# Left operands of the way down summed on VectorE, late differences moved, and attention's convolution and norm in wider instructions

## The chip, the core and the metric

The kernel runs on one core of one Trainium2 chip. The time is that of one execution on the device, in microseconds (us). Before the change the median of three runs was 2420.58 us (2420.09 to 2423.67).

## The reference

One step of a one-layer encoder on two streams: 1024 rows of a new stream, and 64 further rows of a running one that brings 512 cached keys and values, the state of its recurrence, and the last rows ahead of two convolutions. The kernel takes both as T = 1088 columns.

```python
xn = rmsnorm(x)
z, xbc, dt, q, k, v, gate_ssm, gate_att = split(xn @ w_in)
xbc = silu(causal_conv(xbc, 4 taps))                 # 3072 channels
y = ssd_scan(xs, dt, a_neg, bm, cm, state)           # 32 heads, chunks of 64
y = rmsnorm((y + d * xs) * silu(z))
a = softmax(q1 @ k1.T) - lam * softmax(q2 @ k2.T)    # 8 heads, causal by chunks of 64
o = rmsnorm(a @ v, subln_w) * (1 - lambda_init)
x += (sig(gate_ssm) * (y @ w_branch_ssm) + sig(gate_att) * (o @ w_branch_attn)) @ w_out
ha, hb = split(rmsnorm(x) @ w_up)                    # 2 x 2816 channels
x += (silu(causal_conv(ha, 3 taps)) * hb) @ w_down
```

The outputs are x of both streams, the new keys and values, the states, and the last rows ahead of the convolutions, all in float32.

## The kernel before

**How products are made.** Every float32 operand is split into a rounded part hi and a rest lo. A product is then three passes of TensorE: hi by hi, hi by lo, lo by hi, each over a quarter of the columns (QW = 272; HT = 544 is a half). The hi part is a copy on ScalarE (L419), the lo part a subtraction on VectorE (L420); together they are a "split". The large products (input, way up, way down) take two blocks of rows and two halves of the inner dimension at a time and make seven products of them instead of eight. A pair of blocks has 14 steps: product p = 0 to 6, column half s = 0 and 1. For these products both operands need sums and differences of their quadrants:

- The left operands are weights. `make_left` (L551) loads the quadrants of a pair of weight blocks into two buffers (w_f), makes s1 = q21 + q22 (L563), s2 = s1 - q11 (L567), s3 = q11 - q21 (L569) and s4 = q12 - s2 (L565) on GpSimd, and splits what a product needs: wh is a split of products 0 to 3, w_hi and w_lo that of 4 to 6. The rows that s1 and s2 are kept in are named ws1 and ws2. Splits are pinned behind the last evacuation of TensorE's results ("copy" on ScalarE, "read" on VectorE). `lefts_at` says at which of a pair's 14 steps each piece for the next pair is made.
- The right operands are activations of 128 x 1088 elements (a unit of four blocks of 272 columns). In the way down `right_part` loads one of them, and `landed` splits it some steps later, where there are n, m or ph in the rows of the trace. A group of products starts with new right operands.

**The stages.** Input projection with its norm (to about 560 us), attention (560 to 1100), the scan with the products of the branches (1100 to 1560), the output product (to 1730), the way up (1730 to 2160, 22 pairs), and the way down (to 2424, 12 pairs). The way down has three groups of inner blocks, DOWN = (8, 8, 6), with four pairs each; groups are summed up in memory.

**Attention and its filler.** For each of 8 heads there are 9 blocks of 128 query rows (the ninth is the running stream with 64). A block takes: scores on TensorE (sc), a mask and a maximum on VectorE (L1115 or L1116 among them), exponentials on ScalarE (p_t, L1125), the combination of the two softmaxes on VectorE, transpositions on TensorE, copies of them on ScalarE and VectorE (a_t, L1145 and L1147), the product with the values (po, L1160). One block is in flight beside the next one's scores. Between them `fill` puts steps of other products into TensorE's order: the 24 tiles of the scan's input projection with their convolution of four taps (`conv_tiles`, L977), and gates. A tile has four blocks of 272 columns. For each one ScalarE copies the product into pre, makes the first tap (L999), VectorE adds three taps (L1001), then comes silu (L1003) and a store to x_sc in memory. The first three columns of pre come from the block before, by GpSimd (L989). At the end of a head `head_out` scales each of the nine blocks by its norm and by the weight wsub (L1178), transposes them and splits the result (L1189, L1190) into memory. The cached values of the running stream (cv_t) are loaded ahead of a head.

**The way up and down.** In the way up each pair makes a row of h, with a convolution of three taps (L1626 on ScalarE, L1628 on VectorE), and stores it in h_sc. For the way down pairs of rows ("couples") are read back, four differences are made (`differences_of`, L1690: loads at L1694, subtractions at L1698, L1699, L1702 and L1703, stores to t_sc at L1705). Most couples have theirs made in the way up; the last three, whose rows come last, at steps 1, 8 and 10 of the first three pairs of the way down: loads, first two subtractions, other two with the stores. These three are the rows that the third group takes.

`down_pair` (L1720) makes a pair: its passes are L1791, its results are evacuated by ScalarE (products 0 and 2) and VectorE (u at L1796, L1801 and L1805, yq at L1803, L1810 and L1813) and added to the output in memory by GpSimd's DMA queue.

The code gives the order in which work is written. A scheduler then orders it on each engine, with its own estimate of durations and those pins, so a change in one place can move instructions elsewhere.

## Time and profile before

| | |
|---|---|
| runs, median | 2420.58 us (2420.09 to 2423.67) |
| profiled execution, its own time | 2425.83 us |
| its span in the trace | 2424.0 us |
| mean granted clock of TensorE | 0.997 |
| busy: TensorE, VectorE, ScalarE, GpSimd | 98%, 72%, 50%, 30% |
| instructions of the span | 49267 |

A row of a group in the profile reads: line, engine, operation, written tile <- read tiles, size, count; behind the bar the busy time and the mean duration of one in ns; behind the second bar the engine's idle time just before such instructions and what ended most of it. A row of the timeline has the start, the duration and the instruction; in brackets stands the idle time before it and what ended it. A row of waits reads: engine, what waited <- what it waited for, then the sum of us, the count and the longest. Engines are PE (TensorE), PEld (its weight loads), DVE (VectorE), ACT (ScalarE), POOL (GpSimd) and SP (SyncE, which issues most DMAs). The granted clock is a share of full speed.

### The profile page before, as it was taken

The numbers are of one execution on the slowest core, as the hardware profiler recorded it, in microseconds if no ns is written. First come the engines' busy times: TensorE is split into PE (matmuls) and PEld (weight loads), VectorE is DVE, ScalarE is ACT, GpSimd is POOL, SyncE is SP. The second block draws the span as 40 slices with busy tenths as digits, with TensorE's granted clock in tenths as the row PEclk, the third lists the DMA queues.
The fourth block names the chain that finished last, engine by engine and source line by source line (L and its number), as shares of the span: only waits on it lengthen the run. The fifth ranks groups of instructions, "written<-read, shape, count | busy, mean of one in ns | idle before, by whom it ended". The sixth has DMA issues, their size and how long they took to land.

```text
span 2424.0 us, 49267 instructions
## 1 busy us (share of the span) xinstructions
PE 2379.3 (98%) x18648; PEld 2306.1 (95%) x18648; DVE 1750.6 (72%) x3150; ACT 1217.8 (50%) x2695; POOL 731.4 (30%) x773
## 2 busy tenths in 40 slices
PE   8999999999999999999999999999999999999998
PEld 8999999999999999999888899999999999999998
DVE  4678987646868778884789776656866767677765
ACT  6454454325656666665666564334543334352442
POOL 0032433321101101111444442012254455444444
PEclk9999999999999999999999999999999999999999
DMA  7773868536555544435978955764124424367976
GB/s 240 274 245 129 265 218 303 168 104 205 163 157 153 164 143 135 143 104 180 352 264 267 344 190 186 210 208 142 66 82 157 143 98 160 127 199 200 245 182 105
DMA packets 295087, 449.78 MB, mean 186 GB/s; under 512 B 36601, under 2 KB 188290, under 8 KB 294850
## 3 DMA queue, kind: packets, MB, share of 16 engines
q1 hardware_dynamic: 265506, 387.00, 49.5%
q0 software_dynamic: 11040, 26.34, 5.5%
q10 hardware_dynamic: 18304, 33.30, 3.7%
q8 instruction: 146, 2.39, 0.4%
q14 instruction: 91, 0.75, 0.1%
HBM read 294.03 MB, written 152.50 MB: 184 GB/s over the span
## 4 chain that ended last, share of the span: by engine, by line
PE 44%; DVE 6%; DMA 3%; issue 2%; ACT 1%; POOL 1%; SPq 0%; POOLq 0%; DVEq 0%; ACTq 0%
PE mx L1617 13%; PE mx L1791 6%; PE mm L1617 5%; PE mm L170 2%; PE mm L172 2%; PE mm L171 2%; PE mx L170 2%; PE mm L1791 2%; PE mx L172 2%; PE mx L171 2%; PE yi L1306 1%; PE stp L1318 1%; PE ye L1312 1%; DMA b<-y_sc 1%; DMA m_sc<-b_g 1%
## 5 line engine op out<-in xcount | busy, mean ns | idle before, releaser
L170 PE MATMUL mm<-b,w_hi 128*128 128x272 f32 x1376 | 408.7, 297 | 0.0
L172 PE MATMUL mm<-b,w_lo 128*128 128x272 f32 x1376 | 404.2, 294 | 0.0
L171 PE MATMUL mm<-b,w_hi 128*128 128x272 f32 x1376 | 403.0, 293 | 0.0
L170 PEld LDWEIGHTS mm<-b,w_hi 128*128 128x128 f32 x1376 | 259.5, 189 | 5.7 <-issue 3.4
L171 PEld LDWEIGHTS mm<-b,w_hi 128*128 128x128 f32 x1376 | 259.6, 189 | 4.5 <-issue 3.1
L172 PEld LDWEIGHTS mm<-b,w_lo 128*128 128x128 f32 x1376 | 259.1, 188 | 3.6 <-issue 2.5
L1617 PE MATMUL mx<-m,w_hi 128*128 128x272 f32 x792 | 152.3, 290 | 1.2 <-ACT m L419 1.2
L420 DVE TENSOR_TENSOR wh<-w_f,wh 128x512 fp32r<-128x512 f32 (+1 forms) x156 | 151.6, 973 | 0.7 <-ACT wh L419 0.7
L1001 DVE SCALAR_TENSOR_TENSOR cc<-pre,par,cc 128x272 f32<-128x272 f32 (+1 forms) x288 | 139.6, 488 | 9.8 <-ACT cc L999 7.5
L1617 PE MATMUL mx<-n,wh 128*128 128x272 f32 x1056 | 141.6, 288 | 1.1 <-DVE u L1644 1.1
L1125 ACT ACTIVATE p_t<-sc,mx 128x512 f32<-128x512 f32 (+6 forms) x144 | 106.2, 740 | 67.5 <-DVE mx L1116 37.4
L1617 PEld LDWEIGHTS mx<-n,wh 128*128 128x128 f32 x1056 | 135.7, 188 | 1.3 <-DVE u L1644 1.3
L989 POOL COPY pre<-pre 128x3 f32<-128x3 f32 x72 | 27.7, 385 | 346.3 <-DVE cc L1003 182.1
L563 POOL TENSOR_TENSOR ws<-w_f 128x512 f32<-128x512 f32 (+1 forms) x51 | 69.3, 1360 | 198.2 <-DMA w_f<-in_win_dram 82.0
L1617 PEld LDWEIGHTS mx<-m,w_hi 128*128 128x128 f32 x792 | 124.4, 188 | 1.4 <-ACT m L419 1.4
L170 PE MATMUL mx<-b,w_hi 128*128 128x272 f32 x416 | 122.9, 296 | 2.0 <-ACT w_hi L155 1.5
L172 PE MATMUL mx<-b,w_lo 128*128 128x272 f32 x416 | 121.5, 294 | 0.0
L171 PE MATMUL mx<-b,w_hi 128*128 128x272 f32 x416 | 121.4, 292 | 0.0
L1617 PE MATMUL mx<-m,w_lo 128*128 128x272 f32 x396 | 114.2, 289 | 0.0
L1626 ACT ACTIVATE cc<-pre,par 128x544 f32<-128x544 f32 (+1 forms) x44 | 37.2, 846 | 146.2 <-DVE pre L1661 145.3
L156 DVE TENSOR_TENSOR w_lo<-w_f,w_hi 128x1024 fp32r<-128x1024 f32 (+1 forms) x74 | 92.8, 1256 | 22.5 <-ACT w_hi L155 22.1
L419 ACT CAST wh<-w_f 128x512 fp32r<-128x512 f32 (+1 forms) x156 | 95.2, 613 | 27.0 <-POOL w_f L569 8.3
(463 smaller groups left out, 7311.7 us busy)
## 6 DMA issues: line engine op xcount, KB each, us to landing
w_f<-in_win_dram SPq DMA_DIRECT2D x40, 512.0 KB, 4.3
w_f<-in_wup_dram SPq DMA_DIRECT2D x80, 256.0 KB, 2.9
w_f<-in_win_dram SPq DMA_DIRECT2D x76, 256.0 KB, 3.3
bc<-a_sc SPq DMA_DIRECT2D x32, 512.0 KB, 7.1
b<-y_sc SPq DMA_DIRECT2D x24, 544.0 KB, 8.1
h_sc<-hb SPq DMA_DIRECT2D x44, 272.0 KB, 2.1
ht<-h_sc SPq DMA_DIRECT2D x22, 544.0 KB, 4.7
t_sc<-ht SPq DMA_DIRECT2D x22, 544.0 KB, 2.9
```

The costliest lines, as they stand in the source:

```text
L156: V.tensor_tensor(out=lo, in0=w, in1=hi, op=ALU.subtract)
L170: PE.matmul(ps, a_hi, b_hi, start=i == 0, stop=False)
L171: PE.matmul(ps, a_hi, b_lo, start=False, stop=False)
L172: PE.matmul(ps, a_lo, b_hi, start=False, stop=i == n - 1)
L419: S.copy(hi, src)
L420: V.tensor_tensor(out=lo, in0=src, in1=hi, op=ALU.subtract)
L563: G.tensor_tensor(out=s1, in0=q21, in1=q22, op=ALU.add)
L1001: V.scalar_tensor_tensor(cc[:, :m], pre[:, i : i + m], cw(i), cc[:, :m], ALU.mult, ALU.add)
L1125: act(p_t[:n, :nk], sc[c][:n, :nk], AF.Exp, bias=mx[:n, c : c + 1], accum_out=dst)
L1617: PE.matmul(ps, w[x][:, c], b[y][:, k], start=start and k == i == 0, stop=k == 3 and i == 2, skip_group_check=not start)
L1626: act(cc[:, :n], pre[h][:, :n], AF.Identity, bias=col(O_FB + f), scale=cw(0))
L1791: PE.matmul(ps, w[y][:, c], b[z][:, k], start=start and k == j == 0, stop=k == n - 1 and j == 2, skip_group_check=not start)
```

## The change

Five edits, the first two in the way down and the others in attention:

1. For the first pair of each group of the way down (`by_vector`: left operands 22, 26 and 30) the four sums and differences s1 to s4 are made on VectorE, pinned behind the last "copy" and "read", instead of on GpSimd without a pin.
2. The late couples' steps are no longer 1, 8 and 10 in each of the first three pairs, but 5, 11, 13 in the first, 4, 10, 12 in the second and 2, 8, 10 in the third (`LATE`).
3. The convolution of the scan's input works on halves of 544 columns: two blocks of the product are copied into one pre, and then come one first tap, three taps, one silu and one store. pre has two buffers as before, cc two instead of three, each of about twice the size.
4. cv_t has one buffer instead of two, and the cached values of the heads after the first are loaded when the fourth block of the head begins, not before its first.
5. In `head_out` the norm of eight blocks is one multiplication of 128 x 1024 with a broadcast, and a small one for the ninth block. The weight is transposed into a column once (one transposition on TensorE, one copy of a column on ScalarE), and is applied when the transposed rows are split: as the scale of the hi copy on ScalarE and as a factor in the lo subtraction on VectorE.

```diff
+LATE = ((5, 11, 13), (4, 10, 12), (2, 8, 10))
...
-            if what == "s1":
-                G.tensor_tensor(out=s1, in0=q21, in1=q22, op=ALU.add)
...
+            if x in by_vector:
+                with after("copy", "read"):
+                    V.tensor_tensor(out=to, in0=a, in1=b, op=op)
             else:
-                G.tensor_tensor(out=q21, in0=q11, in1=q21, op=ALU.subtract)
+                G.tensor_tensor(out=to, in0=a, in1=b, op=op)
...
+                first = c % HT == 0
+                if first:
+                    pre = cv_pool.tile([P, HT + 6], F32, name="pre", tag="pre", bufs=2)
...
-                cc = cv_pool.tile([P, QW + 3], F32, name="cc", tag="cc", bufs=3)
...
+                if first:
+                    return
...
+                cc = cv_pool.tile([P, HT + 3], F32, name="cc", tag="cc", bufs=2)
...
-            cv_t = ak.tile([P, 4, P], F32, name="cv_t", tag="cv_t", bufs=2)
+            cv_t = ak.tile([P, 4, P], F32, name="cv_t", tag="cv_t")
...
-                cached()
+            later.append(cached)
...
-            for i in range(9):
-                n = min(P, T - i * P)
-                V.scalar_tensor_tensor(o_t[:n, i], o_t[:n, i], rs[:n, i : i + 1], wsub[:n], ALU.mult, ALU.mult)
+            V.tensor_tensor(out=o_t[:, :8], in0=o_t[:, :8], in1=rs[:, :8].unsqueeze(2).to_broadcast([P, 8, P]), op=ALU.mult)
+            V.tensor_scalar(o_t[:TS, 8], o_t[:TS, 8], rs[:TS, 8:9], None, ALU.mult)
...
-                S.copy(hi, pt[:, :w])
-                V.tensor_tensor(out=lo, in0=pt[:, :w], in1=hi, op=ALU.subtract)
+                act(hi, pt[:, :w], AF.Copy, scale=wcol)
+                V.scalar_tensor_tensor(lo, pt[:, :w], wcol, hi, ALU.mult, ALU.subtract)
...
+        pw = pa.tile([P, 512], F32, name="pw", tag="pt", bufs=2)
+        PE.transpose(pw[:, :P], wsub, ident)
+        S.copy(wcol, pw[:, 0:1])
...
+                if x == 3 and later:
+                    later.pop()()
...
+    by_vector = [FT + 4 * g for g in range(len(DOWN))]
...
-            if i in (0, 1, 2) and at in (1, 8, 10):
-                if at == 1:
+            if i in (0, 1, 2) and at in LATE[i]:
+                if at == LATE[i][0]:
```

The lines of the changed kernel are shifted: the sums on VectorE are L567, L420 is L421, the way down's L1791 to L1813 are L1803 to L1825, L1628 is L1640, L1651 to L1661 are L1663 to L1673, and L1698 is L1710.

In VectorE's order at the entry to the way down, before, there stand the splits of the first right operands (n9, n5, n11, m001, m011), the reads of the way up's last pairs (hb, u1 and pre), and two splits of left operands, the one from ws2 (the second product's) and the one from w_f:

```order
L1661 TENSOR_TENSOR pre_27144<-mx_27232,u2_27148 128x272
L420 TENSOR_TENSOR n9_27190<-n9_27190,n8_27189 128x1088
L420 TENSOR_TENSOR n5_27211<-n5_27211,n4_27210 128x1088
L1651 TENSOR_TENSOR u1_27147<-mm_27309,u1_27147 128x272
L420 TENSOR_TENSOR n11_27228<-n11_27228,n10_27227 128x1088
L420 TENSOR_TENSOR wh_27366<-ws2_27282,wh_27366 128x512
L1653 TENSOR_TENSOR hb_27146<-mx_27374,u1_27147 128x272
L420 TENSOR_TENSOR m001_27247<-m001_27247,m000_27246 128x1088
L1655 TENSOR_TENSOR hb_27145<-mx_27394,u1_27147 128x272
L420 TENSOR_TENSOR wh_27388<-w_f_22175,wh_27388 128x512
L420 TENSOR_TENSOR m011_27266<-m011_27266,m010_27265 128x1088
```

At the same place of VectorE's order in the changed kernel:

```order
L1673 TENSOR_TENSOR pre_26612<-mx_26700,u2_26616 128x272
L567 TENSOR_TENSOR ws1_26749<-w_f_21642,w_f_21643 128x512
L421 TENSOR_TENSOR n9_26658<-n9_26658,n8_26657 128x1088
L421 TENSOR_TENSOR n5_26679<-n5_26679,n4_26678 128x1088
L567 TENSOR_TENSOR ws2_26750<-ws1_26749,w_f_21642 128x512
L567 TENSOR_TENSOR w_f_21642<-w_f_21642 128x512
L1663 TENSOR_TENSOR u1_26615<-mm_26777,u1_26615 128x272
L421 TENSOR_TENSOR n11_26696<-n11_26696,n10_26695 128x1088
L421 TENSOR_TENSOR m001_26715<-m001_26715,m000_26714 128x1088
L1665 TENSOR_TENSOR hb_26614<-mx_26842,u1_26615 128x272
L1667 TENSOR_TENSOR hb_26613<-mx_26862,u1_26615 128x272
L421 TENSOR_TENSOR m011_26734<-m011_26734,m010_26733 128x1088
```

Three sums (s1 into ws1, s2 into ws2, s3 into w_f) have come between the splits of right operands, and the split from ws2 has moved from behind n11 to behind m011 and a tap of the last convolution.

On TensorE, where the way down begins in the changed kernel (L1803; L1629 is the way up's last pair), the first product's twelve passes come first, six passes that take the other right operands' tiles for the first time, and the last twelve passes of the way up's last pair:

```order
L1803 MATMUL mx<-ph,wh 128x272 x12
L1803 MATMUL mx<-n_26639,wh 128x272
L1803 MATMUL mx<-n_26640,wh 128x272
L1803 MATMUL mx<-n_26657,w_hi 128x272
L1803 MATMUL mx<-n_26658,w_hi 128x272
L1803 MATMUL mm<-m_26714,w_hi 128x272
L1803 MATMUL mm<-m_26715,w_hi 128x272
L1629 MATMUL mx<-m_21322,w_hi 128x272
L1629 MATMUL mx<-m_21323,w_hi 128x272
```

Before, the twelve passes were followed at once by the rest of the product with n. Six passes and the end of the way up have moved ahead of it.

VectorE's order around the first late couple (ht), before:

```order
L1810 TENSOR_TENSOR yq_27537<-mx_27489,u_27450 128x272
L420 TENSOR_TENSOR n7_27349<-n7_27349,n6_27348 128x1088
L1628 SCALAR_TENSOR_TENSOR cc_27149<-pre_27144,par_81,cc_27149 128x546
L1796 TENSOR_TENSOR u_27451<-mx_27594,u_27450 128x272
L1698 TENSOR_TENSOR ht_27485<-ht_27485 128x544
L1803 TENSOR_TENSOR yq_27554<-mm_27541,u_27450 128x272
L1805 TENSOR_TENSOR u_27451<-mm_27541,u_27451 128x272
```

The same place of VectorE's order in the changed kernel:

```order
L1822 TENSOR_TENSOR yq_27001<-mx_26953,u_26918 128x272
L421 TENSOR_TENSOR n7_26817<-n7_26817,n6_26816 128x1088
L1815 TENSOR_TENSOR yq_27018<-mm_27005,u_26918 128x272
L1817 TENSOR_TENSOR u_26919<-mm_27005,u_26919 128x272
L421 TENSOR_TENSOR m201_26838<-m201_26838,m200_26837 128x1088
L1646 TENSOR_TENSOR hb_26614<-hb_26614,cc_26617 128x480
L1646 TENSOR_TENSOR hb_26614<-hb_26614,cc_26617 128x64
```

The difference (L1698, now L1710) no longer stands ahead of the reads yq and u; it comes nine instructions further on.

VectorE's order at the entry to the second group in the changed kernel, from the last reads of the first group (yq and u) to the second product's split (wh from ws2):

```order
L1825 TENSOR_TENSOR yq_27798<-mx_27785,u_27661 128x272
L567 TENSOR_TENSOR ws1_27800<-w_f_21642,w_f_21643 128x512
L567 TENSOR_TENSOR ws2_27801<-ws1_27800,w_f_21642 128x512
L1808 TENSOR_TENSOR u_27661<-mm_27826,u_27660 128x272
L421 TENSOR_TENSOR ph_27685<-ph_27685,ph_27684 128x1088
L567 TENSOR_TENSOR w_f_21642<-w_f_21642 128x512
L421 TENSOR_TENSOR wh_27840<-w_f_21642,wh_27840 128x512
L421 TENSOR_TENSOR n1_27703<-n1_27703,n0_27702 128x1088
L421 TENSOR_TENSOR wh_27879<-ws2_27801,wh_27879 128x512
```

The other rows stand as before; the three sums have come into them. The fourth (s4) comes eleven rows on, behind the splits of n5 and n11; before, GpSimd made it beside the split of n5.

43 lines of the change are left out of this document (22 added, 21 removed).

## The prediction

> **What bounds the kernel now.** I read the profile from the whole to the single wait: busy times, stages, what TensorE waits for in each stage, and the instructions behind those waits.
>
> ```profile
> PE 2379.3 (98%) x18648; PEld 2306.1 (95%) x18648; DVE 1750.6 (72%) x3150; ACT 1217.8 (50%) x2695; POOL 731.4 (30%) x773
> ```
>
> TensorE is busy for 98% of the span, 2424.0 - 2379.3 = 44.7 us are left. VectorE and ScalarE are not the bound, so what the change takes from them counts only where TensorE stands still for them. The busy time by stage (window, its length, busy us and count of PE, PEld, DVE, ACT, POOL, then the granted clock) shows where that is.
>
> ```profile
> 560.00:1100.00 540.00, 537.24 (x4116) 515.05 (x4115) 432.38 (x1046) 347.00 (x941) 67.39 (x164) 1.00 0.49 150
> 1100.00:1560.00 460.00, 449.60 (x3606) 410.09 (x3606) 337.35 (x464) 263.82 (x619) 163.56 (x108) 1.00 0.78 255
> 1730.00:2160.00 430.00, 430.00 (x3423) 429.97 (x3422) 292.82 (x492) 167.38 (x307) 217.70 (x247) 1.00 0.37 124
> 2160.00:2424.00 264.00, 250.08 (x1952) 248.04 (x1950) 188.27 (x291) 102.92 (x179) 110.85 (x99) 0.98 0.79 197
> ```
>
> Attention (560 to 1100) leaves TensorE 2.8 us idle, the scan 10.4, the way up 0.0, the way down with the drain of the last stores 13.9. The change touches attention and the way down, and through the scheduler the scan's order. The waits of TensorE, in the same order of stages:
>
> ```profile
> PE sc L1111 <- ACT p_t L1125: 1.1, 1, 1.1
> PE po L1160 <- ACT a_t L1145: 0.9, 2, 0.6
> PE po L1160 <- DVE a_t L1147: 0.5, 1, 0.5
> ...
> PE yi L1306 <- DVE y L1314: 3.1, 2, 1.6
> PE tr L1285 <- DVE xx L1294: 2.3, 3, 1.4
> ...
> PE mm L1791 <- DVE n L420: 1.9, 1, 1.9
> PE mm L1791 <- DVE u L1805: 1.5, 1, 1.5
> PE mx L1791 <- DVE u L1796: 0.4, 1, 0.4
> ```
>
> In the way down all waits are for VectorE, and they cost more than they last. Two stretches around them, and one of the way up for comparison (window, length, busy and count of PE, granted clock):
>
> ```profile
> 2171.30:2197.30 26.00, 23.84 (x168) 0.93 0.74 223
> 2264.00:2274.00 10.00, 8.14 (x53) 0.83 1.11 287
> 1740.00:1766.00 26.00, 26.00 (x208) 1.00 0.29 95
> ```
>
> Undisturbed, 208 passes take 26.0 us, 0.125 us each. At the entry to the way down (2171 to 2197) only 168 ran, 40 x 0.125 = 5.0 us late; at the entry to its second group 53 instead of 80, 3.4 us late. Of this the lower clock took 26 x 0.07 = 1.8 us and 10 x 0.17 = 1.7 us. So a wait of 1.5 or 1.9 us brought a second loss of about its own size. [...] In the scan, waits of up to 1.6 us left it at 1.00, so it doesn't always fall.
>
> **Second group: the sums on VectorE.** VectorE, then GpSimd, then TensorE around 2260 us:
>
> ```profile
> 2255.65 2.15 DVE L420 TENSOR_TENSOR ph<-ph 128x1088 fp32r<-128x1088 f32 x1
> ...
> 2262.69 1.27 DVE L420 TENSOR_TENSOR n<-n,n 128x1088 fp32r<-128x1088 f32 x1
> ...
> 2265.53 2.40 DVE L420 TENSOR_TENSOR n<-n,n 128x1088 fp32r<-128x1088 f32 x1
> ...
> 2268.21 0.68 DVE L420 TENSOR_TENSOR wh<-w_f,wh 128x512 fp32r<-128x512 f32 x1
> ```
>
> ```profile
> 2256.73 2.23 POOL L567 TENSOR_TENSOR ws<-ws,w_f 128x512 f32<-128x512 f32 x1
> ...
> 2265.18 1.60 POOL L565 TENSOR_TENSOR w_f<-w_f,ws 128x512 f32<-128x512 f32 x1
> ```
>
> ```profile
> 2267.99 0.39 PE L1791 MATMUL mm<-n,w_hi 128*128 128x272 f32 x1 [1.86 <-DVE n L420]
> ```
>
> A split of 128x1088 takes 1.27 us alone and 2.40 beside a GpSimd sum: VectorE loses 1.1 us for each sum that it meets. The split that TensorE waits for is the one that met the fourth sum (L565). In the change that sum is behind it on VectorE, so the split ends 1.1 us earlier. The other three sums come before; each costs VectorE about 0.6 us (0.68 for a split of the same 512 columns, some 0.08 of it overlapped with the next) instead of 0.9 to 1.1 us of standstill, and VectorE had idle time ahead of the product's read at 2262.34, so their sign hardly counts. The wait falls from 1.86 to about 0.7 us, and I take it that the clock then holds: 1.2 + 1.7 = **2.9 us** gained (bounds: 1.2 if the clock falls all the same, 3.4 if all goes). [...]
>
> **First group: gain and loss.** The rows of VectorE and TensorE at the entry:
>
> ```profile
> 2166.75 2.48 DVE L420 TENSOR_TENSOR n<-n,n 128x1088 fp32r<-128x1088 f32 x2
> ...
> 2170.95 0.69 DVE L420 TENSOR_TENSOR wh<-ws,wh 128x512 fp32r<-128x512 f32 x1
> ...
> 2175.25 1.83 DVE L1628 SCALAR_TENSOR_TENSOR cc<-pre,par,cc 128x544 f32<-128x544 f32 x1
> ...
> 2180.77 0.78 DVE L1628 SCALAR_TENSOR_TENSOR cc<-pre,par,cc 128x544 f32<-128x544 f32 x1
> ...
> 2190.95 1.44 DVE L1698 TENSOR_TENSOR ht<-ht 128x544 f32<-128x544 f32 x1
> 2192.31 0.43 DVE L1803 TENSOR_TENSOR yq<-mm,u 128x272 f32<-128x272 f32 x1
> 2192.66 0.42 DVE L1805 TENSOR_TENSOR u<-mm,u 128x272 f32<-128x272 f32 x1
> ```
>
> ```profile
> 2172.83 1.66 PE L1791 MATMUL mx<-n,wh 128*128 128x272 f32 x12
> ...
> 2193.14 0.73 PE L1791 MATMUL mm<-ph,wh 128*128 128x272 f32 x2 [1.54 <-DVE u L1805]
> ```
>
> The gain: the wait of 1.54 us ends with u (L1805), and the first difference of a late couple (L1698, 1.44 us) stands two instructions ahead of it. In the change it has moved behind the pair yq, u: 1.4 us. The cc of 2175.25 no longer meets a sum, 1.0 us (1.83 against 0.78).
>
> The loss: the split of the second operand (wh from ws), which the second product needs from its third pass on, ends at 2171.64 now. In the change's order, from the end of the read at 2166.75, VectorE has four sums and splits of 512 columns up to and with it (4 x 0.6), five of 1088 (5 x 1.2), three reads (3 x 0.36) and one cc (0.7): 2.4 + 6.0 + 1.1 + 0.7 = 10.2 us, so it ends at about 2176.9. TensorE has 12 passes, then 6, then 12 of the last up pair before it must have it, 30 x 0.125 after 2171.3, so at about 2175.1 (2175.5 with the three passes that also stand ahead): a new wait of **1.4 us**. Adding up the rest of VectorE's list in the same way, TensorE meets two more waits of 0.5 to 0.8 us before it starts the next pair, and is 2.4 to 2.9 us late there instead of 5.0, with the clock held. I take **2.3 us** gained; the bounds are 4.0 (everything but 1 us) and a loss of 1.4 (the new wait in full, nothing given back).
>
> Third group: its only wait is the 0.4 us above. Nothing is counted, within 0.4 us either way. Of the couples' moved steps also the loads (SP's queue) go later; what they write is read again two pairs on, from 2243 us, more than 30 us behind the last step of the first couple, so this is hidden.
>
> **Attention.** VectorE's and ScalarE's groups, with the mean ns of one behind the comma, those of the way up with the doubled width, and a 128x1024 of VectorE:
>
> ```profile
> L1001 DVE SCALAR_TENSOR_TENSOR cc<-pre,par,cc 128x272 f32<-128x272 f32 x213 | 103.4, 487 | 8.9 <-ACT cc L999 7.2
> ...
> L999 ACT ACTIVATE cc<-pre,par 128x272 f32<-128x272 f32 x71 | 43.5, 613 | 8.1 <-DMA x_sc<-cc 3.3 <-POOL pre L989 1.2 <-ACT pre L990 0.4
> ...
> L1178 DVE SCALAR_TENSOR_TENSOR o_t<-o_t,ors,wsub 128x128 f32<-128x128 f32 x56 | 15.4, 342 | 0.1
> ```
>
> ```profile
> L156 DVE TENSOR_TENSOR w_lo<-w_f,w_hi 128x1024 fp32r<-128x1024 f32 x72 | 90.3, 1255 | 22.0 <-ACT w_hi L155 21.6
> ...
> L1628 DVE SCALAR_TENSOR_TENSOR cc<-pre,par,cc 128x546 f32<-128x546 f32 x44 | 37.5, 852 | 1.1 <-ACT cc L1626 0.4
> ...
> L1626 ACT ACTIVATE cc<-pre,par 128x546 f32<-128x546 f32 x22 | 18.6, 846 | 145.3 <-DVE pre L1661 145.3
> ```
>
> The convolution's 96 blocks become 48. Three taps save 3 x 48 x (2 x 0.487 - 0.852) = 17.6 us of VectorE, the first factor 48 x (2 x 0.613 - 0.846) = 18.2 us of ScalarE. The norm's nine products per head (9 x 0.342 = 3.1 us) become one of 128x1024 (1.26 us) and a small one: 8 x 1.6 = 13 us less. The weight rides on the two instructions that split the transposed rows anyway, at no cost that these rows show. But that is some 30 of 432 us on an engine that TensorE waited for 0.5 us here. Only the idle 2.8 us can be won. The longest wait (1.1 us, sc behind p_t, at 1066 us) stands right behind nine norm products; I count that and a part of the rest, **1.5 us** (bounds: 0 and 2.8). Taking cached values at the fourth block into a single buffer costs nothing as long as they land within the five blocks (5 x 540 / 72 = 37 us) that follow. One transposition more at the start is one pass, 0.3 us at most.
>
> **Scan.** No instruction of it changes, but its order on all engines does, since the scheduler starts it from another state. I count 0, with 4 us either way out of its 10.4 us of idle time.
>
> **The sum**: 2.9 + 2.3 + 1.5 = 6.7 us less. The profiled execution took 2425.83 us (span 2424.0), so 2419.1 of such an execution. The median of the runs is 5.25 us below it at 2420.58; carried over, **2413.9 us**. About 0.2% (4.8 us) is what a measurement of this kernel can tell from no change: the marks are 2415.7 and 2425.4.
>
> **The rivals.**
> - *The scan falls better as well* (two of its VectorE waits, 3.1 and 2.3 us, go, or the entry's new wait doesn't arise): 4 us more, 2410. For it: those waits are bare in the trace; against: nothing in the change aims there. 0.2.
> - *VectorE is the bound at both entries and takes the sums' time back*, or the clock falls at the new waits too (2 x 1.7 us): the change does what it says, as the order shows, and gives 2 to 3 us: 2418. For it: between 2166 and 2193 VectorE hardly stands idle. 0.25.
> - *Slower: the wide taps hold softmax back.* A tap lasts 0.36 us longer; an attention block has four VectorE steps in a chain (mask and maximum, reciprocal, combination, copy), each of which finds a tap in front of it about every other time: 4 x 0.5 x 0.36 = 0.7 us later per block. One unit in flight hides it now; if it no longer does in 15 of the 72 blocks, that costs 10 us, and with the gains above, 2424 to 2428, say 2427. It decides from about 15 blocks on. Against it: there are half as many taps, and only five waits now. 0.1.
> - *The forecast*: 0.45, its own range 2411 to 2417.
>
> **Chances.** Faster by over 0.2%: 0.33 of the forecast's 0.45 (the part of its own range below 2415.7), the scan's 0.2 and 0.05 of the second rival's 0.25, together 0.58; within 0.2%: the forecast's other 0.12 and 0.20 of the second rival, 0.32; slower: 0.10. The range leaves out the slowest of the slower case, half of it, and about as much beyond the scan's 2410 - 4: 2406 to 2425.
>
> **What would show it.** Right: no wait for n (L420) above 1 us and a granted clock near 1.00 around the second group's start; a wait for wh (from ws) at the first product pair of about 1.4 us; no wait behind a late couple's difference; idle TensorE time in attention below 2 us. Wrong: a clock still at 0.83 to 0.93 at the entries, more waits for maxima or p_t in attention, or a scan whose idle time differs from 10.4 by more than 4 us.

## The result, and the profile after

The changed kernel takes 2437.90 us (median of six runs, 2434.35 to 2439.68), before takes 2421.47 (six runs, 2420.09 to 2424.81): 1.0064 of before, interval 1.0051 to 1.0077. The medians are 16.4 us apart; by the ratio the change is 0.64% slower, where 6.7 us less was forecast.

The profiled execution has a span of 2436.7 us against 2424.0. Its page, engine by engine (busy us, share, instructions):

```profile
PE 2380.8 (98%) x18649; PEld 2308.3 (95%) x18649; DVE 1729.7 (71%) x2914; ACT 1202.4 (49%) x2600; POOL 682.1 (28%) x713
```

TensorE does the same work, VectorE, ScalarE and GpSimd do less, and the span is 12.7 us longer. (Before's profiled execution, 2425.83 us, was slower than its six runs above, the changed kernel's, 2438.51, was near its median; so the stages add up to 12.7 us and not to 16.4.) To see where, take the first and last instruction of a kind as the ends of a stage: scores (sc) for attention, transpositions of the scan (tr), the way down's first and last passes. Each row gives the count, shortest, median and longest ns, and the first and last start. Before:

```profile
L1111 PE MATMUL sc<-kh,q x208: 191/341/500, 566.0 to 1095.7; 128*128 128x512 f32 x73, 128*128 128x384 f32 x8, 128*128 128x256 f32 x8, 128*64 128x64 f32 x8
...
L1285 PE MATMUL tr<-con,in x144: 270/273/331, 1127.8 to 1464.8; 128*128 128x128 f32 x128, 128*64 128x128 f32 x16
...
L1791 PE MATMUL mx<-ph,wh x135: 282/287/293, 2171.3 to 2404.5; 128*128 128x272 f32 x135
...
L1791 PE MATMUL mx<-m,w_lo x105: 285/290/296, 2184.3 to 2413.9; 128*128 128x272 f32 x105
```

The same rows of the changed kernel:

```profile
L1118 PE MATMUL sc<-kh,q x208: 191/341/501, 564.7 to 1091.2; 128*128 128x512 f32 x73, 128*128 128x384 f32 x8, 128*128 128x256 f32 x8, 128*64 128x64 f32 x8
...
L1297 PE MATMUL tr<-con,in x144: 270/272/476, 1122.4 to 1474.2; 128*128 128x128 f32 x128, 128*64 128x128 f32 x16
...
L1803 PE MATMUL mx<-ph,wh x135: 283/287/293, 2179.3 to 2417.6; 128*128 128x272 f32 x135
...
L1803 PE MATMUL mx<-m,w_lo x105: 284/289/296, 2195.2 to 2427.0; 128*128 128x272 f32 x105
```

Attention went from 529.7 to 526.5 us, 3.2 less. From its last scores to the scan's last transposition it was 369.1 and is 383.0: **13.9 more**. The way down was 242.6 and is 247.7: **5.1 more**. (1.3 less came ahead of attention and 1.4 less between the scan's last transposition and the way down. In seven profiles with the same order of work there, before and e2, e5, e6, e9, e10 and e18 below, these two stretches differ by 4.6 and 2.2 us.) TensorE's longest waits in the changed kernel, from attention on:

```profile
PE tr L1297 <- DVE xx L1306: 4.7, 1, 4.7
PE mx L1803 <- ACT w_hi L420: 4.0, 2, 3.5
PE tr L1297 <- DMA in<-x_sc: 3.9, 1, 3.9
...
PE mx L1803 <- DVE yq L1822: 3.2, 1, 3.2
...
PE mm L1803 <- DVE w_lo L421: 2.0, 1, 2.0
...
PE mx L1803 <- DVE wh L421: 1.2, 1, 1.2
```

The waits that the change was aimed at (n at L420, u behind the late couple) are gone. Others have come, two of them in the scan, of which no instruction was edited.

**The way down.** VectorE, then ScalarE, in the first pair of the second group:

```profile
2277.91 0.68 DVE L567 TENSOR_TENSOR w_f<-w_f,ws 128x512 f32<-128x512 f32 x1
2278.51 0.68 DVE L421 TENSOR_TENSOR w_lo<-w_f,w_hi 128x512 fp32r<-128x512 f32 x1
2279.11 0.68 DVE L421 TENSOR_TENSOR w_lo<-ws,w_hi 128x512 fp32r<-128x512 f32 x1
```

```profile
2283.97 1.10 ACT L420 CAST n<-n 128x1088 fp32r<-128x1088 f32 x1 [4.65 <-DMA n<-h_sc]
...
2286.38 0.61 ACT L420 CAST w_hi<-w_f 128x512 fp32r<-128x512 f32 x1
```

TensorE in the way down:

```profile
2201.36 0.49 PE L1803 MATMUL mx<-m,w_hi 128*128 128x272 f32 x2 [3.23 <-DVE yq L1822]
...
2252.46 0.39 PE L1803 MATMUL mx<-n,wh 128*128 128x272 f32 x1 [1.15 <-DVE wh L421]
...
2279.25 0.40 PE L1803 MATMUL mm<-ph,w_lo 128*128 128x272 f32 x1 [2.00 <-DVE w_lo L421]
...
2287.05 0.52 PE L1803 MATMUL mx<-n,w_hi 128*128 128x272 f32 x2 [3.51 <-ACT w_hi L420]
```

The fourth sum (L567 at 2277.91) no longer stands beside a split that TensorE waits for. But it is late itself, and two operands are made behind it: w_lo, 2.00 us late, and the split of s4. Its hi copy (w_hi from w_f) now stands behind copies of right operands on ScalarE, and ScalarE waited 4.65 us for the DMA of one of them: 3.51 us late, although s4 had been ready for 7.8 us.

VectorE at two other places of the way down, and GpSimd at the same times:

```profile
2195.43 1.46 DVE L1640 SCALAR_TENSOR_TENSOR cc<-pre,par,cc 128x546 f32<-128x546 f32 x1
...
2197.16 1.43 DVE L421 TENSOR_TENSOR wh<-w_f,wh 128x512 fp32r<-128x512 f32 x1
2198.52 2.35 DVE L421 TENSOR_TENSOR m<-m,m 128x1088 fp32r<-128x1088 f32 x1
...
2245.93 3.78 DVE L1711 TENSOR_TENSOR ht<-ht 128x544 f32<-128x544 f32 x1 [1.18 <-DMA ht<-h_sc]
```

```profile
2194.71 1.59 POOL L569 TENSOR_TENSOR ws<-w_f 128x512 f32<-128x512 f32 x1 [18.01 <-DVE hb L1646]
2196.38 1.67 POOL L569 TENSOR_TENSOR ws<-ws,w_f 128x512 f32<-128x512 f32 x1
2198.00 1.71 POOL L569 TENSOR_TENSOR w_f<-w_f 128x512 f32<-128x512 f32 x1
...
2246.28 1.57 POOL L569 TENSOR_TENSOR ws<-ws,w_f 128x512 f32<-128x512 f32 x1
2247.53 1.58 POOL L569 TENSOR_TENSOR w_f<-w_f 128x512 f32<-128x512 f32 x1
```

VectorE comes to the read (yq) that TensorE waits for at 2201 only 21.4 us after the way down's first pass; before it was 15.0 (2186.30 against 2171.3). Ahead of it there are now the four sums of the first pair, and in the new order also the two splits shown, which met the second pair's sums on GpSimd and took 1.43 and 2.35 us where they take 0.68 and 1.28 alone. And a step of the third couple (ht, 0.72 us alone) ran into two sums in a row and took 3.78 us; the 1.15 us at 2252 stand behind it.

**The scan.** From attention's last scores to the last transposition TensorE runs the same 2914 passes, but stands idle for 18.2 us instead of 8.3. The other 4 us are longer busy time, at a granted clock of 0.98 instead of 1.00. Two of VectorE's three longest products of decay and scores, and GpSimd beside them:

```profile
1179.66 4.49 DVE L1310 TENSOR_TENSOR bc<-bc,b_cb 128x1024 f32<-128x1024 f32 x1
...
1289.02 7.62 DVE L1310 TENSOR_TENSOR bc<-bc,b_cb 64x512 f32<-64x512 f32 x1 [0.66 <-issue]
```

```profile
1179.30 3.76 POOL L1345 TENSOR_TENSOR y<-y,zin 128x1536 f32<-128x1536 f32 x1
...
1286.85 3.47 POOL L1345 TENSOR_TENSOR y<-y,zin 128x1536 f32<-128x1536 f32 x1
1290.28 1.04 POOL L1335 TENSOR_TENSOR state<-state,decs 128x512 f32<-128x512 f32 x1
1291.27 1.09 POOL L1307 TENSOR_SCALAR_AFFINE_SELECT bc<-bc 128x1024 f32<-128x1024 f32 x1
1292.33 1.81 POOL L1347 TENSOR_TENSOR zin<-zin 128x768 f32<-128x768 f32 x1
1294.09 1.04 POOL L1335 TENSOR_TENSOR state<-start,decs 128x512 f32<-128x512 f32 x1
1295.09 1.00 POOL L1348 TENSOR_TENSOR zin<-zin 128x384 f32<-128x384 f32 x1
```

VectorE's instruction at 1289.02 lasts 7.62 us, through the six of GpSimd's from 1286.85 on, which run without a gap, and ends 0.5 us after the sixth.

### The profile page after: what moved, and what is told of

Read it like the earlier page. It is cut to its first block, busy times and chain, and to the rows that moved or that the text cites. A ratio compares the mean times of both kernels' runs of the same rounds, so it can differ in the third digit from the quotient of the medians.

```text
span 2436.7 us, 48641 instructions
## 1 busy us (share of the span) xinstructions
PE 2380.8 (98%) x18649; PEld 2308.3 (95%) x18649; DVE 1729.7 (71%) x2914; ACT 1202.4 (49%) x2600; POOL 682.1 (28%) x713
## 4 chain that ended last, share of the span: by engine, by line
PE 50%; DMA 4%; DVE 4%; issue 2%; ACT 1%; POOL 1%; POOLq 0%; SPq 0%; DVEq 0%; ACTq 0%
PE mx L1629 13%; PE mx L1803 5%; PE mm L1629 5%; PE mm L171 4%; PE mm L172 4%; PE mm L173 4%; PE mx L171 3%; PE mx L173 3%; PE mx L172 2%; PE mm L1803 2%; PE yi L1318 1%; PE stp L1330 1%; PE po L1167 1%; PE ye L1324 1%; DMA t_sc<-ht 1%
## 5 line engine op out<-in xcount | busy, mean ns | idle before, releaser
L1629 PE MATMUL mx<-m,w_hi 128*128 128x272 f32 x792 | 152.3, 289 | 1.2 <-ACT m L420 1.2
L421 DVE TENSOR_TENSOR wh<-w_f,wh 128x512 fp32r<-128x512 f32 (+1 forms) x156 | 144.7, 928 | 0.8 <-ACT wh L420 0.7
L1629 PE MATMUL mx<-n,wh 128*128 128x272 f32 x1056 | 141.6, 288 | 1.1 <-DVE u L1656 1.1
L1629 PEld LDWEIGHTS mx<-n,wh 128*128 128x128 f32 x1056 | 135.7, 188 | 1.3 <-DVE u L1656 1.3
L1629 PEld LDWEIGHTS mx<-m,w_hi 128*128 128x128 f32 x792 | 124.4, 188 | 1.4 <-ACT m L420 1.4
L1009 DVE SCALAR_TENSOR_TENSOR cc<-pre,par,cc 128x544 f32<-128x544 f32 (+1 forms) x144 | 111.2, 772 | 8.2 <-ACT cc L1007 6.9
L1629 PE MATMUL mx<-m,w_lo 128*128 128x272 f32 x396 | 114.1, 289 | 0.0
L420 ACT CAST wh<-w_f 128x512 fp32r<-128x512 f32 (+1 forms) x156 | 95.3, 613 | 26.8 <-POOL w_f L569 8.2
L1646 POOL TENSOR_TENSOR hb<-hb,cc 128x544 f32<-128x544 f32 (+2 forms) x63 | 67.1, 1078 | 135.5 <-DVE hb L1667 101.2
```

The source lines that it names most:

```text
L420: S.copy(hi, src)
L421: V.tensor_tensor(out=lo, in0=src, in1=hi, op=ALU.subtract)
L1009: V.scalar_tensor_tensor(cc[:, :m], pre[:, i : i + m], cw(i), cc[:, :m], ALU.mult, ALU.add)
L1629: PE.matmul(ps, w[x][:, c], b[y][:, k], start=start and k == i == 0, stop=k == 3 and i == 2, skip_group_check=not start)
L1646: (V if f + 1 == FT else G).tensor_tensor(out=hb[h][:, o : o + n], in0=hb[h][:, o : o + n], in1=cc[:, d : d + n], op=ALU.mult)
```

## The experiments

All ratios are to the kernel before on the same chip, with their 95% intervals. "Attention", "scan" and "way down" are the three stretches defined above, in us, from one profiled execution each. Most of these are near the median of their runs; e3's was the slowest of its runs (5.4 us above the median), those of e7, e9, e11 and e12 the fastest (7.1, 4.0, 4.2 and 3.3 us below). The last column says with which kernel a run shares its order of work in the scan, compared instruction by instruction from the first to the last transposition on TensorE, VectorE, ScalarE and GpSimd. The stretch "scan" holds 2914 passes of TensorE before; it holds 2961 in e11 and e12, 2903 in e13 and e17, and 2896 in e4.

| run | ratio (interval) | attention | scan | way down | order of the scan |
|---|---|---|---|---|---|
| before | | 529.7 | 369.1 | 242.6 | before |
| changed | 1.0064 (1.0051 to 1.0077) | 526.5 | 383.0 | 247.7 | changed |
| e1 attention's edits | 1.0040 (1.0027 to 1.0053) | 526.5 | 381.5 | 241.0 | changed |
| e2 way down's edits | 1.0034 (1.0020 to 1.0047) | 530.1 | 367.7 | 247.8 | before |
| e3 wide convolution | 1.0048 (1.0036 to 1.0060) | 527.0 | 386.2 | 241.1 | own |
| e4 norm | 1.0000 (0.9990 to 1.0010) | 530.3 | 371.7 | 242.0 | own |
| e5 sums on VectorE | 1.0043 (1.0031 to 1.0055) | 529.7 | 368.8 | 248.7 | before |
| e6 late couples | 1.0020 (1.0011 to 1.0029) | 530.5 | 368.4 | 246.8 | before |
| e7 gate product on VectorE | 1.0066 (1.0051 to 1.0081) | 526.5 | 376.7 | 248.0 | own |
| e8 gate product in four | 1.0058 (1.0045 to 1.0072) | 526.5 | 376.8 | 248.8 | own |
| e9 first couple only | 1.0013 (1.0004 to 1.0021) | 529.0 | 368.1 | 244.1 | before |
| e10 sums without s4 | 1.0002 (0.9994 to 1.0011) | 530.8 | 368.0 | 242.6 | before |
| e11 before, rate 1.20 | 1.0037 (1.0025 to 1.0049) | 529.7 | 374.5 | 240.9 | own |
| e12 e1, rate 1.20 | 1.0063 (1.0051 to 1.0074) | 526.6 | 384.0 | 240.7 | own |
| e13 wide in 18 tiles | 1.0025 (1.0014 to 1.0036) | 527.3 | 380.3 | 240.4 | shared with e17 |
| e14 wide in 6 tiles | 1.0075 (1.0063 to 1.0087) | 537.2 | 380.8 | 240.8 | changed |
| e15 e1, rate 1.16 | 1.0046 (1.0033 to 1.0059) | 526.5 | 380.5 | 240.5 | own |
| e17 narrow, two cc | 1.0061 (1.0049 to 1.0074) | 537.1 | 377.5 | 241.0 | shared with e13 |
| e18 groups 2 and 3, no s4 | 0.9986 (0.9976 to 0.9995) | 528.7 | 370.2 | 240.6 | before |

Length of some pairs of the way down, from the start of the pair's first pass to that of the next (168 passes each, 126 in the third group; undisturbed 21.0 and 15.8 us):

| run | 1st | 3rd | 4th | 5th (second group) | 9th (third group) |
|---|---|---|---|---|---|
| before | 27.8 | 21.2 | 21.2 | 24.7 | 16.2 |
| e1, e3, e4, e11 to e15, e17 (way down not edited) | 26.1 to 28.9 | 21.1 to 22.7 | 21.1 | 22.5 to 23.2 | 16.0 to 16.3 |
| changed | 27.7 | 21.2 | 22.6 | 28.8 | 15.8 |
| e5 sums on VectorE | 30.3 | 21.2 | 21.1 | 28.7 | 15.8 |
| e6 late couples | 25.2 | 23.8 | 24.3 | 25.9 | 16.1 |
| e9 first couple only | 25.2 | 22.6 | 22.7 | 26.0 | 16.0 |
| e10 sums without s4 | 30.0 | 21.2 | 21.2 | 22.6 | 16.0 |
| e18 groups 2 and 3, no s4 | 28.0 | 21.4 | 21.1 | 22.3 | 16.2 |

The 24.7 us of before's fifth pair are not what this way down usually takes. In before's profile the clock is halved there (0.50 from 2269 to 2271, 0.83 over 10 us); in none of the nine other profiles with an unedited way down is it lowered in this pair, and they take about 23.0 us. Their whole way down takes 240.4 to 242.0 us.

### Which edits carry the loss: e1 to e4

e1 has the edits of attention alone, e2 those of the way down alone.

```diff
-LATE = ((5, 11, 13), (4, 10, 12), (2, 8, 10))
...
-    by_vector = [FT + 4 * g for g in range(len(DOWN))]
```

> The three edits of attention alone (wide convolution, one buffer of cached values, norm and weight), the way down as before; its order up to the way down is that of the changed kernel on every engine. Theory A (the scan's new order costs more than attention gains, because VectorE's products of decay and scores, bc, meet GpSimd's long products more often): attention 4 to 5 us shorter, the scan 13 to 15 us longer, way down as before, so 2428 to 2432 us. Theory B (the way down's edits carry the loss, the longer scan is scatter between executions): within 3 us of before, 2418 to 2424.

> The two edits of the way down alone (sums on VectorE, late couples moved); its order up to the way down is that of before. Theory A: only the way down changes, 4 to 6 us longer, 2425 to 2427 us, with the wait for w_hi of about 3.5 us in the second group's first pair, the one for yq of about 3 us at 2200, and one behind a late couple's difference. Theory B: the whole loss, 2434 to 2438.

e1 took 2432.55 us against 2422.55, e2 2429.20. The loss adds up from two halves that know nothing of each other: in e1 the scan is 12.4 us longer, in e2 the way down 5.2. Their 0.40% and 0.34% make 0.74, against 0.64 (0.51 to 0.77) for the whole. The longer scan is no scatter, since e1 repeats it in another execution of the same order. Theory A held as to the places; its sizes were a little off (e1's attention is 3.2 us shorter, not 4 to 5, and e2's median 2 us above its range).

e3 leaves out the norm's edit, e4 has it alone:

> The wide convolution with the single buffer of cached values, without the norm's edit. Attention 2 to 4 us shorter by both theories. Theory A: the scan gets a third order and moves by an amount that follows the time by which VectorE's instructions are lengthened in the scan (43.8 us before, 56.7 us in the changed kernel): for each us of that about 1 us of the scan. Theory C (the scan is longer because it starts earlier and then waits for its DMAs): the scan ends where it ended before, so 2419 to 2422.

> The norm's edit alone (one product of 128 x 1024, weight as a column). Attention 0 to 2 us shorter. Theory A: a fourth order of the scan; its length again follows how much VectorE's instructions are lengthened in it. Theory C: 2419 to 2422, since the scan starts at most 2 us earlier.

The loss comes with the convolution and the single buffer of cached values, which e3 has together (386.2 us). The norm's edit alone changes nothing that can be measured in the time (2422.23 against 2422.55), although its scan has an order of its own, and little in attention. Theory C failed for e3: its scan starts 6.6 us earlier and ends 10.5 us later than before's.

### The way down taken apart: e5, e6, e9, e10

```diff
-            if i in (0, 1, 2) and at in (1, 8, 10):
+            if i in (0, 1, 2) and at in LATE[i]:
```

> Only the sums of the first left operand of each group on VectorE; the late couples stay at steps 1, 8 and 10. Theory A1 (the sums' place, pinned behind the reads and copies, makes the last operands late: w_lo behind s4 on VectorE, and w_hi behind copies of right operands on ScalarE that wait for their DMAs): the waits of 2.0 and 3.5 us of the second group's first pair are here too and the way down is 247 to 250 us (241 to 243 with the way down of before), 2426 to 2429 in all. Theory A2 (the moved couples cost it, since they fall among GpSimd's sums of the next pair): way down within 1.5 us of 242.

> Only the late couples moved. Theory A1: the wait of 1.5 us behind the first couple's difference goes, a wait of at most 1.2 us comes where the third couple meets GpSimd's sums: way down 240 to 242 us, 2419 to 2422 in all. Theory A2: way down 246 to 249, 2425 to 2428.

Both parts cost, and not the sum: e5 2429.88 us and e6 2426.05 against 2421.92. With the sums on VectorE alone the first pair and the fifth are longer (30.3 and 28.7); with the couples moved alone the first is 2.6 us shorter, as intended, and the third to fifth give back 2.6, 3.1 and 1.2 (2.9 against the usual 23.0). On e5 theory A1's numbers came (248.7 us for the way down; the time of 2429.88 is just above its range), on e6 theory A2's (246.8 us and 2426.05). Each theory named one part, and both are true.

e10 leaves s4 where it was:

```diff
-            if x in by_vector:
+            if x in by_vector and what != "s4":
```

> The kernel before with s1, s2 and s3 of each group's first left operand on VectorE, but s4 on GpSimd and without its pin, as it was. Theory A1 (s4's place behind the splits makes the last operand late): the waits for w_lo (2.0 us) and w_hi (2.0 to 3.5 us) of the second group's first pair go, the first pair of that group takes 23 to 25 us instead of 28.7, the way down 242 to 245. Rival (VectorE simply has no time for the sums there): it stays at 27 us or more, and the way down at 247 to 249.

Its waits of TensorE in the way down:

```profile
PE mx L1790 <- DVE yq L1809: 3.7, 1, 3.7
PE mx L1790 <- ACT w_hi L419: 0.8, 2, 0.4
```

The fifth pair falls from 28.7 to 22.6 us: the place of s4 alone made the loss there. That is 2.1 us below before's profile, but only 0.4 below what this pair usually takes. The wait for yq in the first pair remains (3.7), so that is the work of the other three sums.

e9 moves only the first couple:

```diff
+LATE = ((5, 11, 13), (1, 8, 10), (1, 8, 10))
```

> The kernel before with only the first late couple moved (5, 11, 13 in the first pair; the other two stay at 1, 8, 10). From the starts of the pairs' passes in the way down: with all three couples moved the first pair took 25.2 us instead of 27.8, but the third and fourth 23.8 and 24.3 instead of 21.1 each. Theory A2 (each couple's place acts on its own pair and the next): the first pair 25.2, all others as before, the way down 239 to 241 us, 2.6 us off the time: 2417 to 2420. Rival (the gain in the first pair is given back behind it): way down 242 or more, 2421 or more.

The first pair keeps its gain (25.2) and the third to fifth lose 1.4, 1.5 and 1.3 (3.0 against the usual 23.0): the rival held, 2425.76 us against 2423.76. The couples after it stand at the same steps as before; that they meet other work there is likely, and not shown by itself.

### The scan: e7, e8, e11 to e15, e17

e7 moves the gate product from GpSimd to VectorE, e8 cuts it in four on GpSimd; both on the changed kernel.

```diff
-            G.tensor_tensor(out=y, in0=y, in1=zt, op=ALU.mult)
+            V.tensor_tensor(out=y, in0=y, in1=zt, op=ALU.mult)
```

> The changed kernel with one instruction of the scan moved: the product of y and the gate (128 x 1536, 12 of them, 3.5 us each) on VectorE instead of GpSimd. Theory A (the scan's loss is VectorE shut out behind this GpSimd product): no VectorE instruction of the scan lasts over 3 us, and the time by which VectorE's are lengthened there falls from 56.7 us to 30 or less; the scan is 368 to 374 us long instead of 383, and the kernel 2422 to 2430 us. Theory D (the order of TensorE's work in the scan is what costs, the transpositions standing ahead of the products that they wait with): the scan stays at 380 us or more, and the time within 4 us of 2438.

> The changed kernel with the same product still on GpSimd, in four instructions of 128 x 384 in a row. It asks whether VectorE gets in between two GpSimd instructions. Theory A, if VectorE may start at the end of any GpSimd instruction: the longest VectorE instructions of the scan fall from 7.6 and 4.5 us to 2.5 or less, and the scan to 370 to 376 us. Theory A, if VectorE stays shut out as long as GpSimd has another instruction ready (as the product of 7.62 us that lasted through six of GpSimd's suggests): they still last 3.5 us and more, and the scan stays at 378 to 386. Theory D: 380 or more as well, whatever their lengths.

VectorE's products of decay and scores in the scan, before:

```profile
L1298 DVE TENSOR_TENSOR bc<-bc,b_cb 128x1024 f32<-128x1024 f32 x32 | 48.4, 1511 | 20.2 <-ACT bc L1297 11.5 <-ACT b_cb L1290 8.6
```

In the changed kernel:

```profile
L1310 DVE TENSOR_TENSOR bc<-bc,b_cb 128x1024 f32<-128x1024 f32 x32 | 59.8, 1870 | 12.9 <-ACT bc L1309 8.4 <-ACT b_cb L1302 4.5
```

In e7:

```profile
L1310 DVE TENSOR_TENSOR bc<-bc,b_cb 128x1024 f32<-128x1024 f32 x32 | 42.5, 1328 | 11.5 <-ACT b_cb L1302 5.9 <-ACT bc L1309 5.5
```

The mean went from 1.51 us to 1.87, and in e7 to 1.33: the shut-out is real, and both runs take most of it away. No VectorE instruction of the scan lasts over 2.5 us in e7 or over 2.3 in e8. The scan is 6 us shorter than the changed kernel's in both profiles, below theory D's 380 us and above theory A's 374 and 376. The time does not follow: e7's median is 2436.82 us against 2421.92, and its profiled execution, at 2429.69, was the fastest of six, so its 376.7 us flatter it; e8 took 2434.06, and neither ratio differs from the changed kernel's by more than the intervals. Theory A falls as the whole explanation. What the shut-out costs by itself is not shown, since both runs also have another order of the scan, from 1155 and 1161 us on.

e11 and e12 change only the rate of other work in the scan, on before and on e1; e15 does so by the smallest step.

```diff
-SCAN_STEPS = 1.17
+SCAN_STEPS = 1.20
```

> The kernel before, where only the rate at which other products are put between the scan's steps is 1.20 instead of 1.17. The same work and the same attention, another order of the scan. Theory D (before's order in the scan is a picked one; another order, whatever it comes from, costs 7 us or more): the scan from its first to its last transposition takes 345 us or more instead of 337, 2428 us or more. Theory E (it is the wide convolution that makes the scan longer, by its earlier start or its other timing): within 4 us of before, 2418 to 2426.

> The three edits of attention alone, with the same rate of 1.20. Theory D: yet another order, its scan differs from the 350 us of the 1.17 version by 4 us or more in either direction. Theory E: 347 to 354 us as with 1.17, and the time 2429 to 2435.

> The three edits of attention alone, with the rate of other work in the scan at 1.16 instead of 1.17: the smallest step that gives the scan another order. Theory D: its scan differs from 350 us by 3 us or more. Theory E: 347 to 354 us.

e11 took 2433.83 us against 2423.76: with not one instruction changed, only their order, before loses 10 us. But it does not lose them in the scan. From first to last transposition it has 342.3 us (1125.4 to 1467.7), short of the 345 that theory D asked for, and its 5.4 us more of scan are 47 passes more (2961 against 2914; at 0.125 us each 5.9 us), which the higher rate takes earlier. For the same work this scan is as long as before's. The loss stands behind it, where TensorE waits for the last step of the scan on GpSimd, at 1497 us:

```profile
PE gst L1340 <- POOL zin L1336: 7.7, 2, 7.2
```

The row counts two such waits; the one at 1497 us lasts 7.2. Before, other passes fill this place, and no wait is shown there. From 1490 to 1504 us e11's clock is 0.63 besides. e12 took 2439.51, with the same work moved and the same wait (6.9 us), and 353 us between its first and last transposition; e15 took 2434.57, with 349.5 us. Theory E's numbers came in both: with the edits of attention the scan stays long at all three rates.

e13 and e14 make only some of the 24 tiles wide:

```diff
+            wide = HT if (f in group(3)) == WIDE_LAST else QW
```

> The three edits of attention alone, with the wide convolution only for the first eighteen tiles; the last six, which run just ahead of the scan, are in blocks of 272 columns as before. Theory F (what the scan starts from at the end of attention makes it longer): from its first to its last transposition 336 to 341 us, as with the narrow convolution, 2416 to 2422 in all. Theory E (the wide convolution anywhere): 347 to 354 us and 2429 to 2435. Theory D (every order has its own length, wide or narrow): something between.

> The counterpart: only the last six tiles wide. Theory F: 347 to 354 us for the scan and 2430 to 2436 in all. Theory E: between, nearer to 340. Theory D: another value again, not tied to the place of the wide tiles.

From the first to the last transposition e13 has 351.3 us, against theory F and as theory E says; e14 has 349.7, as theory F says and against theory E (its time, 2441.61 us, is above what both say). Neither theory holds for both. e14's attention is 7.5 us longer than before's. In the scan it has the order of the changed kernel and of e1, although eighteen of its tiles are narrow, and it has their length (351.8 and 350.0 us).

What e13 and e14 share with all the others of the long scan is the pool, two buffers for cc instead of three, and the single buffer of cached values with its later loads. e17 keeps both and has no wide instruction at all:

```diff
-                cc = cv_pool.tile([P, QW + 3], F32, name="cc", tag="cc", bufs=3)
+                cc = cv_pool.tile([P, HT + 3], F32, name="cc", tag="cc", bufs=2)
```

> The norm's edit and the single buffer of cached values, the convolution in blocks of 272 columns throughout, but with the buffers of the wide one: two for cc instead of three. No instruction is wide here; only the count of buffers differs from the norm's edit alone, whose time was that of before. Theory G (with two cc buffers a convolution waits for the one before it, and this gives the orders that end badly in the scan): from attention's last scores to the scan's last transposition 378 us or more, instead of 368 to 372, and 2428 us or more. Theory E (the wide instructions): 368 to 374 us, 2418 to 2425.

ScalarE's first taps in e4, which has three buffers for cc, and in e17:

```profile
L999 ACT ACTIVATE cc<-pre,par 128x272 f32<-128x272 f32 x72 | 44.1, 613 | 8.7 <-DMA x_sc<-cc 4.1 <-POOL pre L989 0.9 <-issue 0.4
L1009 ACT ACTIVATE cc<-pre,par 128x272 f32<-128x272 f32 x72 | 44.1, 613 | 35.3 <-DMA x_sc<-cc 31.6 <-POOL pre L996 0.9 <-POOL pre L991 0.7
```

2439.02 us against 2423.94: as slow as the changed kernel, without its wide instructions, but only in part by the same way. Half is lost in attention (537.1 us, 6.8 more than e4). There ScalarE waits 31.6 us for the stores that free a buffer of cc, instead of 4.1, and TensorE's idle time goes from 1.5 to 7.9 us, with waits for ScalarE ahead; nothing waits for the cached values. This is theory G's mechanism, and e14 has it too (27.7 us); the changed kernel does not have it, its ScalarE waits for no store there. The other half is lost in the scan (377.5 us, 5.8 more than e4, at the edge of theory G's 378). There e17 has the order of e13, whose first eighteen tiles are wide, and nearly its length (348.5 and 351.3 us from first to last transposition). So the long scan needs no wide instruction. Which of the two things that e17 and the others share brings these orders, the buffers of cc or the single buffer of cached values, was not separated: e17 differs from e4 in both, and not in the count of cc's buffers alone.

### The part that gains: e16 and e18

```diff
+    by_vector = [FT + 4 * g for g in (1, 2)]
```

> The kernel before with s1, s2 and s3 on VectorE for the second and the third group only, s4 on GpSimd. From the runs with these parts: first pair of the way down 27.8 as before, the second group's first pair 22.6 instead of 23.0 to 24.7, the third's 15.8 to 16.0 instead of 16.2. Theory A1: 0.5 to 2.4 us off the way down, 2419 to 2422 in all. Rival: nothing of it is left behind the pairs, 242 us or more for the way down.

> The kernel of e16 once more, for a profile of an ordinary execution and more executions: the second group's first pair 22.6 us, the way down 240 to 242, 0 to 3 us under before. Rival as there: 242 or more, and no difference from before.

e16 has 0.9991 of before (0.9981 to 1.0001). Its profiled execution took 5931.63 us, more than twice all others of the same kernel (2417.74 to 2425.20), and is not used. e18, the same kernel, took 2420.46 us against 2423.94, 0.9986 (0.9976 to 0.9995), with the fifth pair at 22.3 us. Its waits in the way down:

```profile
PE mm L1790 <- DVE u L1804: 1.5, 1, 1.5
...
PE mx L1790 <- DVE n L420: 0.4, 1, 0.4
```

The wait for n, which was 1.9 us in before's profile and 0.5 to 1.2 in the nine others with an unedited way down, is 0.4. This is the only version here that beats before, by 0.14% (0.05 to 0.24), and the changed kernel by about 18 us. The profiles do not show where: 240.6 us of way down are what those nine have as well.

## Why the prediction was wrong, step by step

- **Scan (forecast 0, 4 either way; measured 13.9 us more).** The step that failed. "No instruction of it changes" was true, and worth nothing: the order did change, and the scan's length goes with it. From the first to the last transposition the seven profiles with before's order have 335.2 to 338.0 us. The three with the changed kernel's order (changed, e1, e14) have 349.7 to 351.8, although e14's attention is another one and 10.7 us longer. The bound of 4 us came from the 10.4 us of idle time that a better order could save, and bounded the gain; nothing bounded the loss. That idle time (1100 to 1560 us) is 19.4 us in the changed kernel, one of the prediction's own signs of being wrong. The rival of a better scan got 0.2, a worse one was not among the rivals. It is not shown that any other order is longer: e4 has one of its own in before's time, and e11's scan is as long as before's for the same work.
- **Second group (forecast 2.9 us of gain; measured 4.1 of loss in its first pair).** The split of n did escape the fourth sum, as argued. The step stopped there, without asking who reads s4. What reads it are the last product's w_lo and w_hi, and the hi copy fell behind copies on ScalarE that wait for DMAs (4.65 us for one of them). e10 shows that this made the loss: with s4 left on GpSimd the pair takes 22.6 us. The gain was taken too high as well. It was read from one profile, and 1.7 of the 2.9 us are its halved clock, which the nine other profiles with an unedited way down do not have here. Against their 23.0 us there were at most 2.0 to win, and the loss is 5.8.
- **First group (forecast 2.3; measured 0.1).** Two terms, both real, cancel: the moved couple gains 2.6 us (e6, e9; I had 1.4 of it, and the freed tap), the three sums cost 2.2 to 2.5 (e5, e10). The forecast priced the new wait at the split of the second operand (1.4 us; it is not among the waits of over 1 us) and missed a read 20 us further on, yq, that comes 6.4 us later in VectorE's list.
- **The other couples (forecast nothing).** Only their loads were followed through the queue. What counts is whom VectorE meets: a subtraction of 0.72 us took 3.78 beside GpSimd's sums, and the fourth pair is 1.4 us longer.
- **Third group (nothing within 0.4):** right, 0.4 us less.
- **Attention (forecast 1.5, bounds 0 and 2.8; measured 3.2).** Right in kind, and beyond its own bound. TensorE's idle time from the first to the last scores fell from 2.6 to 0.6 us; the rest of the 3.2 us is shorter busy time, which the forecast did not look for. It came with the convolution (e3: 527.0 us) and not with the norm (e4: 530.3), behind whose products the forecast had seen the longest wait. TensorE's one wait left there of those shown before is this:

```profile
PE sc L1118 <- ACT p_t L1132: 0.5, 1, 0.5
```

- **The slower rival** (wide taps hold softmax back) did not happen: the loss had another place. The chance of 0.10 for slower was given to the wrong mechanism, and the range ended 13 us short of the median.

What stays open: why the orders that come with the edits of attention other than the norm have the longer scan, in all seven that were run (345.5 to 355.4 us from first to last transposition). e7 and e8 show that the shut-out of VectorE is not all of it, e14 and e17 that it does not hang on how many tiles are wide, e12 and e15 that another rate does not undo it. The buffers of cc and the single buffer of cached values were not taken apart. That the order is worse is shown; what makes the scheduler choose it is not. A kernel with the wide convolution and before's order of the scan was not tried, since the scheduler sets the order.

## What to carry to other kernels

In a kernel whose order comes from a scheduler and has been tuned by its constants, a change in one stage reorders the stages behind it, and here the order cost more than the saved instructions gave: price "other order" as a loss too. Before a longer stage is called slower, count whether it holds the same work; in e11 it did not. When a sum is moved to another engine to free a split, follow its result to the next reader, and that reader's queue, before counting the gain. Take the base of a forecast from several profiles: before's alone showed a halved clock that the others did not have. And move one part at a time: of the five edits here one part of one is a small gain by itself, and the rest buried it.

## What the runs showed of the hardware

VectorE's instruction of 64x512, 0.67 us at its shortest (e7), took 7.62 us while GpSimd ran six instructions without a gap, and ended 0.5 us after the last of them. It is not always so. In e8 a product of 128x1024 on VectorE (1.88 us, from 1243.81) began 0.8 us before GpSimd's four instructions in a row ended, and ended 1.1 us into GpSimd's next one.

The granted clock does not go by the length of a wait alone. Windows of the changed kernel around its waits (window, length, TensorE busy and count, clock, share of DMA, GB/s):

```profile
1184.00:1198.00 14.00, 9.04 (x53) 0.76 1.05 363
1288.00:1302.00 14.00, 7.70 (x50) 0.76 0.57 191
2198.00:2210.00 12.00, 8.77 (x71) 1.00 0.42 111
2276.00:2292.00 16.00, 10.49 (x70) 0.89 1.08 317
```

The wait of 3.23 us at 2201 left it at 1.00, as did those of 1.15 and 2.00 us; after the one of 3.51 us it was lower (16 us at 0.89), around those of 4.68 and 3.85 us in the scan too (14 us at 0.76 each). In before's profile it fell after waits of 1.54 us (0.50 from 2194 to 2196) and 1.86 us (0.50 from 2269 to 2271); at the second of these places the nine other profiles with an unedited way down, with waits of 0.5 to 1.2 us, kept it at 1.00. What decides when it falls is not shown. In the prediction, 1.7 us of clock were added to a wait of 1.9 us; the runs show that such a term does not go with a wait's length alone.
